# Hybrid attention and convolution layer: bias tiles loaded straight from the tables, convolution steps and bias tables moved to other steps

## The chip, the cores and the metric

One core of one Trainium2 chip runs one program. The metric is device time in microseconds (us), from the first to the last instruction with the little that lies around it; lower is better. Five engines work side by side, each through its own queue in order: TensorE (PE: matmuls; PEld is its weight load), VectorE (DVE), ScalarE (ACT), GpSimd (POOL) and SyncE (SP), which here issues nearly all DMA transfers.

## The reference

One layer over 2048 latent tokens (a grid of 32 rows by 64 columns) and 256 context tokens, width 1024, all in float32:

```python
hx = modulate(rms_norm(x, norm1_g[i]), sh1, sc1)         # hc: the same for ctx
qx, kx, vx, ux = split_proj(hx @ w_in[i])                # 8 heads of 64; u has 1024 columns
attn_x = neighbourhood_attention(rot(qx), qx, rot(kx), vx, kc, vc, rpb[i])
conv_x = conformer_conv(ux, dw_kernel[i], dw_bias[i], conv_ln_g[i], conv_ln_b[i])
x = x + g1 * (concat(attn_x, conv_x) @ w_out[i])
x = x + g2 * (square(relu(modulate(rms_norm(x, norm2_g[i]), sh2, sc2) @ w1)) @ w2)
return rms_norm(x, final_g)
```

Attention: each token sees a window of 8 rows by 16 columns with a learned bias per head (`rpb`, 15 x 31 values a head) and all 256 context keys, in one softmax. Convolution: `a * sigmoid(b)` of u's halves, a depthwise convolution of width 31 over the tokens, a layer norm over 512 channels, silu.

## The kernel before

Every float32 matmul is made of three (`mm3`, L89 to L92): each operand is split into a rounded high part and a low part, high by ScalarE or VectorE, low by a subtraction on VectorE or POOL.

**Projection.** The 2048 tokens are two blocks of 1024, each of two halves of 512 tokens. Each block has ten groups of 256 weight columns: four u groups (they feed the convolution), two q, two k and two v. A step is one group over one half, `half(gi, hf)` at L710; the list at L852 makes 40 steps of them, numbers 0 to 39 (block one: u is 0 to 7, q 8 to 11, k 12 to 15, v 16 to 19; block two the same with 20 more, its v steps interleaved). A q or k step has 48 matmuls of 512 columns; then `rope_store` (L576) rotates its result out of PSUM: VectorE's shuffle (L585) and product (L594), the high and low parts of q and of rotated q (L606, L607, on ScalarE, VectorE and POOL), and eight stores to DRAM. Its tiles come from the ring "G" of four buffers (`gtile`), as do u's gated products, the squares' scratch and the bias tables' tiles.

PSUM is one tile of four slots of 1024 columns. `psA` (L54) hands them out in turn, by the order in which the program is written; one slot is held by the convolution from step 5 on, so three go round. A matmul into a slot waits until all readers of its former content are done. Which ready instruction an engine takes next is fixed when the program is built, by a scheduler with a timing model: program order is the priority, and what isn't ready by the model is passed over.

**Convolution.** 21 blocks of 98 tokens (class `Conv`, L418), each a transform of 128 tokens by matmuls: `load` (cw from h_d), `split`, `fwd` (three matmuls, then y = result x table into the tile cy, its high part cyh on ScalarE and low part cyl on VectorE, L435 to L439), and in the step behind it `inv` (six matmuls, layer norm into co) and two steps behind `turn` (four transposes, silu into ccx, store to cv_d). `conv_end` at a step's end does split and fwd of the present block and loads the next; `conv_at` in the step does turn of the last but one and inv of the last. The blocks 0 to 9 begin at the end of step 7 and go through steps 8 to 16, the blocks 10 to 20 from step 27 to 37. `fwd`'s and `inv`'s results share the held slot.

**Bias tables.** `bias_start` (step 6) spreads rpb in DRAM (z_d). `bias_head` (steps 8 to 15, one a head: q and k of block one) loads two shifted views, adds the column mask on POOL (L287), and stores the head's tables: tf_d has 15 relative rows of 40 columns for 32 query columns, ti_d 14 rows, masked at both ends. `bias_rows(i)` (steps 18, 20, 21, 24) copies from them, DRAM to DRAM, what query row i of four needs, into bias_d: by type of row group (first, middle, last) a [16, 4, 32, n] array, n = 320 or 440. Attention then takes one bias tile, 128 partitions (4 query rows x 32 columns), with one load.

**Attention.** 64 pairs p (4 head pairs `pr` x 8 groups of four grid rows `g` x 2 column halves `hf`), two heads each, in a software pipeline written out by `CYCLE` and `NEED` (L1134, L1141). `addmax` (L1035) adds the bias tile to the scores in PSUM and finds the largest; then exponential, sum, normalising, transposes, product with v. SP's loads are put out by `loads(p)` (L1157): bias and q three pairs ahead, v two, the next head pair's k along the way. A bias tile serves all pairs of one (head pair, hf, type, head): 48 loads in all, 12 a head pair, all at its change, into a ring of eight tiles that come from the weights' ring "W". The outputs go to DRAM (at_d) for the output projection; the MLP follows (from about 990 us on).

**Other pieces the change touches.** `ada_chunk` (L484) makes a modulation row piecemeal on VectorE; its `finish` sums over partitions on TensorE into PSUM, loads the row of b_ada (L517) and adds it (L518). `norm_half` (L545) scales four tiles of x on VectorE and adds the shift on POOL (L221); they are transposed on TensorE (L227) before they can be multiplied.

Of the kernel before, what the change touches and what calls it, by code (L numbers as in the profile page):

```python
# [10 lines left out]
F32 = mybir.dt.float32  # L11
# [7 lines left out]
P = 128  # L19
D = 1024  # L20
# [6 lines left out]
PAD = CW // 2  # L27
# [5 lines left out]
BLK = 1024  # L33
NB = S // BLK

CL = P - CW + 1
# [5 lines left out]
def hybrid_layer(ctx: ExitStack, tc: tile.TileContext, a: dict, out: bass.AP):  # L42
# [68 lines left out]
    ti_d = dr.tile([8, 2, 32, 14 * 40], F32, name="ti_d")  # L111

    bias_d = [dr.tile([16, 4, 32, n], F32, name=f"bias_d{i}") for i, n in enumerate((320, 440, 320))]

# [186 lines left out]

    def bias_rows(i):
        for ty, t, o, n in ((0, tf_d, 7 - i, 320), (1, ti_d, 3 - i, 440), (2, tf_d, 3 - i, 320)):
            SY.dma_start(bias_d[ty][:, i], t.rearrange("h f c n -> (h f) c n")[:, :, o * 40:o * 40 + n])


# [111 lines left out]
    class Conv:  # L418
# [12 lines left out]
        def fwd(self):  # L431
            i, hl, o = self.i, cvc["hl"], cvc["ps"][:, 0:512]
            mm3(o, hl[:, 0, 0:P], hl[:, 1, 0:P], self.w[:, 1, :], self.w[:, 0, :], True, True)
            y = pa.tile([P, 2, 512], F32, tag="acc", bufs=2, name=f"cy{i}")
            VE.tensor_tensor(y, o.unsqueeze(1).broadcast_to([P, 2, 512]), cvc["ab"], ALU.mult)  # L435
            self.yh = pa.tile([P, 2, 512], F32R, tag="H", bufs=3, name=f"cyh{i}")
            self.yl = pa.tile([P, 2, 512], F32R, tag="H", bufs=3, name=f"cyl{i}")
            SE.copy(self.yh, y)
            VE.tensor_tensor(self.yl, y, f(self.yh), ALU.subtract)  # L439
# [24 lines left out]
    cvs = [Conv(i) for i in range(NCB)]  # L464
    cv_pos = [0]

    def conv_at(d, last):
        i = cv_pos[0] - d  # L470
        if 0 <= i < last and not hasattr(cvs[i], f"did{d}"):
            setattr(cvs[i], f"did{d}", True)
            (Conv.inv, Conv.turn)[d - 1](cvs[i])

    def conv_end(last):
        i = cv_pos[0]
        if i < last:
            cvs[i].split()
            cvs[i].fwd()
            if i + 1 < last:  # L480
                cvs[i + 1].load()
        cv_pos[0] += 1

    def ada_chunk(ch):  # L484
# [8 lines left out]
        def step(i):  # L493
# [11 lines left out]
            else:  # L505
                VE.scalar_tensor_tensor(acc, r, sil[:, k:k + 1], acc, ALU.mult, ALU.add)
            if i == 2 * KD:
                pe_todo.append(finish)

        def finish():  # L510
            acc = box["a"]
            pg = psA(f"pg{ch}")
            for n in range(2):
                TE.matmul(pg[0:1, n * 512:(n + 1) * 512], ones[:, 0:1], acc[:, n * 512:(n + 1) * 512],
                          start=True, stop=True)
            br = pa.tile([1, D], F32, tag="m1", bufs=2, name=f"br{ch}")
            SY.dma_start(br, a["b_ada"][:, ch * D:(ch + 1) * D])  # L517
            VE.tensor_tensor(br, pg[0:1, :], br, ALU.add)  # L518
# [26 lines left out]
    def norm_half(tiles, b, hf):  # L545
        scale, shift = norm_mod(tiles, Ar, Br, f"n{b}{hf}")
        for i in range(4):
            scale(i)
            shift(i)
        return tiles  # L550
# [128 lines left out]
    NG = len(groups)  # L679
    CB0 = (BLK - P + PAD) // CL + 1  # L680
    CBS = (CB0, NCB)
    BR0 = 9
    adas = {ch: ada_chunk(ch) for ch in (2, 3, 4)}
    G0 = NG // NB
    ADA = {G0 - 1: 2, G0: 3, G0 + 2: 4}
# [24 lines left out]
    def half(gi, hf):  # L710
# [3 lines left out]
        if kind == "u":  # L714
            ct = idx
            pt = psA(f"pu{b}{ct}{hf}")
            for t in range(4):
                for k in range(KD):
                    wh, wl = wget(k, slice(0, 2 * P))
# [7 lines left out]
            SY.dma_start(h_d[t0:t0 + 512, ct * P:(ct + 1) * P].rearrange("(t p) c -> p t c", p=P), sg)  # L727
            if ct == 3 and hf == 1:
                cv_pos[0] = (0, CB0)[b]
                cvs[cv_pos[0]].load()  # L730
                conv_end(CBS[b])
        elif kind in "qk":
            pt = psA(f"p{kind}{b}{idx}{hf}")
            for j in range(2):
                conv_at(2 - j, CBS[b])
                for k in range(KD):
                    lh, ll = wget(k, slice(j * P, (j + 1) * P))
                    mm3(pt[:, j * 512:(j + 1) * 512], lh, ll, thv[:, k, :], tlv[:, k, :], k == 0, k == KD - 1)
            rope_store(b, kind, idx, hf, pt)
            conv_end(CBS[b])  # L740
        else:
            for t2 in range(2):
# [3 lines left out]
                row = (b * BLK + hf * 512 + t2 * 256) // W  # L746
                conv_at(2 - t2, CBS[b])
                if idx == 1 and hf == 1 and b + 1 < NB:
                    trans_half(pend["x"], b + 1, 0, (2 * t2, 2 * t2 + 1))
                v_tiles([getter(2 * t2), getter(2 * t2 + 1)], row, wget, idx, f"{b}{idx}{hf}{t2}")  # L750
            conv_end(CBS[b])
        if gi == 1 and hf == 0:
# [11 lines left out]
        if gi == 0 and hf == 1:  # L764
# [7 lines left out]
            for i in range(2):  # L772
                scale(i)
                shift(i)
                SY.dma_start(xc_d[i * P:(i + 1) * P, :], ts_[i])
        if gi == 3 and hf == 0:
            bias_start()
            bias_end()
        if 4 <= gi < 8:
            bias_head((gi - 4) * 2 + hf)  # L780
        if gi == 1 and hf == 1:
            conv_loads()
        if gi == 2 and hf == 1:
            conv_tables()
        if hf == 0 and BR0 <= gi < BR0 + 4:
            bias_rows(gi - BR0)
        todo, pe_todo[:] = list(pe_later), list(pe_todo)
# [69 lines left out]
    steps[-4:] = [(NG - 2, 0), (NG - 1, 0), (NG - 2, 1), (NG - 1, 1)]  # L857
    for i, (gi, hf) in enumerate(steps):

        for nxt, nh in steps[i + 1:i + 3]:  # L860
# [137 lines left out]
    def load_b(pr, hf, g, hd):  # L998
# [8 lines left out]
        nw = nr * 40  # L1007
        SY.dma_start(bt[:, SC0 - nw:SC0], bias_d[ty][h * 2 + hf].rearrange("i c n -> (i c) n"))
        BT[key] = bt
# [599 lines left out]
```

## Time and profile before

| | |
|---|---|
| runs | 2570.44, 2568.53, 2560.25 us; median 2568.53 |
| profiled execution | 2570.69 us; span 2568.9 us; mean granted TensorE clock 0.979 |
| PE busy | 2430.5 us (95%) |
| DVE / ACT / POOL busy | 1790.2 (70%) / 1248.7 (49%) / 1467.8 (57%) us |
| DMA | 387.26 MB, mean 151 GB/s |

How to read it: busy time is a sum over the whole span, and TensorE's matmuls overlap, so a busy TensorE isn't one at its peak. The granted clock is the share of TensorE's full clock (2.4 GHz; the lower level is 1.2) in a stretch. Stretches of the span: start and block one's u steps to 158 us, its q steps to about 252, k to 290, v to 348; block two's u to 459, q, k and v to 665; attention to 932.

### The profile page before, as it was taken

How to read it: one execution, taken by the hardware profiler on the slowest of the kernel's cores; microseconds unless marked ns; L12 is line 12 of the kernel's file. 1: busy time of each engine (PE TensorE's matmuls, PEld its weight loads, DVE VectorE, ACT ScalarE, POOL GpSimd, SP SyncE). 2: the span in 40 equal slices, each digit the busy share in tenths (PEclk: the TensorE clock that was granted, in tenths of full speed). 3: DMA queues.
4: the chain of work that ended last, by engine and by line, in shares of the span. 5: the costliest groups of instructions: out<-in, count | busy, mean ns of one | idle time of the engine just before them, and what ended most of it. 6: DMA issues, size and time to landing. Idle time of an engine off the chain costs nothing.

```text
span 2568.9 us, 42313 instructions
## 1 busy us (share of the span) xinstructions
PE 2430.5 (95%) x15903; PEld 2216.9 (86%) x15903; DVE 1790.2 (70%) x2465; ACT 1248.7 (49%) x2162; POOL 1467.8 (57%) x1055
## 2 busy tenths in 40 slices
PE   7997989899889999988999999999999999999997
PEld 5985889689889999987998889999889998799996
DVE  6646743666689976468666697666786676876676
ACT  4334531443689963134444554444554445454442
POOL 3537422442578856457555676555675556755564
PEclk9998999999999999999999999999999999999999
DMA  8555764653899865665333443333343334433321
GB/s 299 158 168 163 223 216 130 196 154 110 227 253 262 241 182 174 195 231 165 99 99 107 129 139 111 101 105 99 121 148 101 99 99 126 137 107 100 105 92 57
DMA packets 293882, 387.26 MB, mean 151 GB/s; under 512 B 38021, under 2 KB 231228, under 8 KB 293644
## 3 DMA queue, kind: packets, MB, share of 16 engines
q1 hardware_dynamic: 293660, 384.54, 49.7%
q8 instruction: 125, 2.05, 0.3%
q14 instruction: 81, 0.66, 0.1%
q10 hardware_dynamic: 16, 0.00, 0.0%
HBM read 308.03 MB, written 86.76 MB: 154 GB/s over the span
## 4 chain that ended last, share of the span: by engine, by line
PE 62%; DVE 10%; DMA 9%; POOL 5%; issue 4%; SPq 2%; ACT 1%; DVEq 0%; POOLq 0%; ACTq 0%
PE pall L90 18%; PE pall L91 18%; PE pall L92 18%; PE pall L1105 2%; PE pall L1069 1%; PE pall L1030 1%; DVE s L1398 1%; DMA ar<-at_d 1%; DVE ac L1501 1%; DVE ac L1497 1%; PE pall L1107 1%; DVE w L1423 1%; PE pall L1032 1%; DMA cw<-h_d 1%; DMA xn_d<-xo 1%
## 5 line engine op out<-in xcount | busy, mean ns | idle before, releaser
L90 PE MATMUL pall<-w,hh 128*128 128x512 f32 x1024 | 406.0, 397 | 11.0 <-DVE ac L1497 7.2
L91 PE MATMUL pall<-w,hh 128*128 128x512 f32 x1024 | 403.0, 394 | 0.0
L92 PE MATMUL pall<-w,hl 128*128 128x512 f32 x1024 | 397.2, 392 | 0.6 <-DVE hl L1454 0.6
L1497 DVE TENSOR_TENSOR ac<-pall,ac 128x1024 f32<-128x1024 f32 x239 | 286.8, 1214 | 73.9 <-PE pall L92 73.2
L90 PEld LDWEIGHTS pall<-w,hh 128*128 128x128 f32 x1024 | 195.1, 190 | 51.6 <-issue 4.4
L92 PEld LDWEIGHTS pall<-w,hl 128*128 128x128 f32 x1024 | 193.3, 189 | 41.9 <-DVE hl L1454 2.2
L91 PEld LDWEIGHTS pall<-w,hh 128*128 128x128 f32 x1024 | 194.8, 190 | 36.4 <-issue 0.2
L1451 ACT ACTIVATE c<-c 128x512 f32<-128x512 f32 x128 | 80.9, 632 | 157.2 <-DVE c L1471 129.2
L86 POOL TENSOR_TENSOR w_0l<-w_0r,w_0h 128x1024 fp32r<-128x1024 f32 x20 | 50.7, 2537 | 172.7 <-ACT w_0h L85 152.5
L90 PE MATMUL pall<-xah,w 128*128 128x256 f32 x512 | 144.8, 284 | 4.7 <-ACT w L1392 4.7
L92 PE MATMUL pall<-xah,w 128*128 128x256 f32 x512 | 145.2, 284 | 0.0
L91 PE MATMUL pall<-xal,w 128*128 128x256 f32 x512 | 145.0, 283 | 0.0
L1454 DVE TENSOR_TENSOR hl<-c,hh 128x512 fp32r<-128x512 f32 x128 | 123.7, 967 | 15.3 <-ACT hh L1453 15.2
L1062 POOL TENSOR_SCALAR sb<-sb,ri 128x696 f32<-128x696 f32 (+1 forms) x128 | 105.6, 826 | 49.7 <-DVE ri L1057 40.7
L1044 DVE CUSTOM_DVE_ANT_0 sb<-pall,bias 128x696 f32<-128x696 f32 (+1 forms) x128 | 108.0, 845 | 6.5 <-PE pall L1032 5.9
L1052 ACT ACTIVATE sb<-sb,mn 128x696 f32<-128x696 f32 (+1 forms) x128 | 109.6, 857 | 0.6 <-DVE mn L1044 0.6
L90 PEld LDWEIGHTS pall<-xah,w 128*128 128x128 f32 x512 | 98.1, 192 | 7.5 <-ACT w L1392 4.9
L91 PEld LDWEIGHTS pall<-xal,w 128*128 128x128 f32 x512 | 98.6, 192 | 2.8
L92 PEld LDWEIGHTS pall<-xah,w 128*128 128x128 f32 x512 | 98.6, 192 | 2.1
L90 PE MATMUL pall<-xth,w 128*128 128x256 f32 x256 | 75.2, 294 | 19.1 <-DVE pu L1459 19.1
L1105 PE MATMUL pall<-pw,v 120*128 120x256 f32 (+1 forms) x480 | 90.8, 309 | 0.8 <-ACT ob L1112 0.8
L1081 DVE TENSOR_TENSOR pw<-pall,pw 120x512 fp32r<-120x512 f32 (+1 forms) x128 | 83.5, 653 | 5.1 <-ACT pw L1076 4.7
(853 smaller groups left out, 8797.0 us busy)
## 6 DMA issues: line engine op xcount, KB each, us to landing
v<-v_d SPq DMA_DIRECT2D x144, 120.0 KB
q<-q_d SPq DMA_DIRECT2D x64, 256.0 KB
wr<-in_w_ada SPq DMA_DIRECT2D x48, 256.0 KB
v_d<-vt SPq DMA_DIRECT2D x64, 160.0 KB
wa<-in_w_ada SPq DMA_DIRECT2D x8, 1024.0 KB
x<-in_x SPq DMA_DIRECT2D x16, 512.0 KB
kr<-k_d SPq DMA_DIRECT2D x32, 256.0 KB
at_d<-ao SPq DMA_DIRECT2D x32, 256.0 KB
```

Of the source, the lines that this page charges most:

```text
L86: (eng or GE).tensor_tensor(l, r, f(h), ALU.subtract)
L90: TE.matmul(outp, lh, rh, start=start, stop=False)
L91: TE.matmul(outp, lh, rl, start=False, stop=False)
L92: TE.matmul(outp, ll, rh, start=False, stop=stop)
L1044: VE.tensor_tensor_reduce(sb[:, c0:SE_], d["s"][:, 512 - SC0 + c0:768], bt[:, c0:SE_], -1.0, 3e38, ALU.add, ALU.min, mn)
L1052: SE.activation(pb[:, c0:SE_], pb[:, c0:SE_], AF.Exp, bias=d["mn"], scale=-1.0, accum_out=d["sm"])
L1062: GE.tensor_scalar(pb[:, c0:SE_], pb[:, c0:SE_], d["ri"], 1.0, ALU.mult, ALU.mult)
L1081: VE.tensor_tensor(pw[0:120, 0:nch, 1, :], d["tv"], f(pw)[0:120, 0:nch, 0, :], ALU.subtract)
L1105: TE.matmul(o, VT[(pr, *key)][0:n, hd, :], pw[0:n, ch, :, :], start=(ch == 0), stop=False)
L1451: SE.activation(c, c, AF.Relu)
L1454: VE.tensor_tensor(dl, cv, f(dh), ALU.subtract)
L1497: VE.tensor_tensor(ac, po_, ac, ALU.add)
```

## The change

1. `bias_d` and `bias_rows` are gone; `load_b` loads a bias tile with four transfers of 32 partitions, one a query row, straight from tf_d or ti_d.
2. `bias_start` and `bias_end` run in step 17 (before: 6), `bias_head` in steps 20 to 27, the u steps of block two (before: 8 to 15).
3. The convolution blocks are put to steps by a table, `ENTER`: blocks 0 to 7 at steps 12 to 19, 8 and 9 at steps 22 and 24, 10 to 20 at steps 27 to 37. u steps call `conv_at` too. The first block's tile is loaded at the end of the step before.
4. `cy` is a PSUM slot by `psA` and no longer an SBUF tile.
5. `ada_chunk` loads its row of b_ada when its last step is put out, not in `finish`.
6. For block two's second half, two of the four shifts of `norm_half` go to VectorE.

```diff
-    bias_d = [dr.tile([16, 4, 32, n], F32, name=f"bias_d{i}") for i, n in enumerate((320, 440, 320))]
-    def bias_rows(i):
-        for ty, t, o, n in ((0, tf_d, 7 - i, 320), (1, ti_d, 3 - i, 440), (2, tf_d, 3 - i, 320)):
-            SY.dma_start(bias_d[ty][:, i], t.rearrange("h f c n -> (h f) c n")[:, :, o * 40:o * 40 + n])
...
-            y = pa.tile([P, 2, 512], F32, tag="acc", bufs=2, name=f"cy{i}")
+            y = psA(f"cy{i}").rearrange("p (z n) -> p z n", z=2)
...
+    now = [0]
+    def conv_at(d):
+        i = ENTER.get(now[0] - d)
+        if i is not None:
             (Conv.inv, Conv.turn)[d - 1](cvs[i])
+    def conv_end():
+        i = ENTER.get(now[0])
+        if i is not None:
             cvs[i].split()
             cvs[i].fwd()
+        i = ENTER.get(now[0] + 1)
+        if i is not None:
+            cvs[i].load()
...
             if i == 2 * KD:
+                box["b"] = pa.tile([1, D], F32, tag="m1", bufs=2, name=f"br{ch}")
+                SY.dma_start(box["b"], a["b_ada"][:, ch * D:(ch + 1) * D])
                 pe_todo.append(finish)
...
-            br = pa.tile([1, D], F32, tag="m1", bufs=2, name=f"br{ch}")
-            SY.dma_start(br, a["b_ada"][:, ch * D:(ch + 1) * D])
+            br = box["b"]
...
-            shift(i)
+            shift(i, VE if b and hf and i % 2 else GE)
...
+    ENTER = {n: i for i, n in enumerate([*range(12, 20), 22, 24, *range(27, 38)])}
...
             for t in range(4):
+                if t % 2 == 0:
+                    conv_at(2 - t // 2)
...
-        if gi == 3 and hf == 0:
+        if gi == G0 - 2 and hf == 1:
             bias_start()
             bias_end()
-        if 4 <= gi < 8:
-            bias_head((gi - 4) * 2 + hf)
+        if G0 <= gi < G0 + 4:
+            bias_head((gi - G0) * 2 + hf)
...
-        if hf == 0 and BR0 <= gi < BR0 + 4:
-            bias_rows(gi - BR0)
...
-        SY.dma_start(bt[:, SC0 - nw:SC0], bias_d[ty][h * 2 + hf].rearrange("i c n -> (i c) n"))
+        t, o = ((tf_d, 7), (ti_d, 3), (tf_d, 3))[ty]
+        for i in range(4):
+            SY.dma_start(bt[i * 32:i * 32 + 32, SC0 - nw:SC0], t[h, hf][:, (o - i) * 40:(o - i) * 40 + nw])
```

## Rows read from the trace of the kernel before

**Rows 1.** Stretches: length, busy us of PE, PEld, DVE, ACT, POOL; clock; DMA.
```profile
185.50:260.00 74.50, 55.83 (x224) 43.36 (x223) 45.68 (x53) 33.45 (x64) 55.40 (x31) 0.84 0.57 161
303.00:348.00 45.00, 41.83 (x340) 40.59 (x339) 19.42 (x32) 19.71 (x36) 4.77 (x2) 1.00 0.96 312
372.00:392.00 20.00, 13.72 (x84) 13.08 (x85) 12.49 (x8) 4.65 (x5) 11.61 (x4) 0.74 0.05 14
...
686.00:726.00 40.00, 40.00 (x321) 39.55 (x320) 39.90 (x100) 37.03 (x80) 34.86 (x50) 1.00 0.98 255
726.00:766.00 40.00, 33.38 (x246) 31.82 (x245) 30.87 (x81) 29.88 (x66) 24.84 (x39) 0.96 1.02 250
790.00:822.00 32.00, 30.61 (x248) 30.18 (x247) 29.69 (x81) 28.88 (x66) 25.23 (x39) 1.00 1.08 253
```

**Rows 2.** Timeline of TensorE, 185 to 262 us: start, length, instruction, [idle before <-releaser].
```profile
202.53 0.50 PE L90 MATMUL pall<-cw,chl 128*128 128x512 f32 x1 [3.26 <-ACT ccx L460]
214.45 0.48 PE L91 MATMUL pall<-cyl,chl 128*98 128x512 f32 x1 [1.51 <-DVE cyl L439]
236.12 0.56 PE L458 MATMUL pall<-ident,co 98*128 98x98 f32 x4 [2.31 <-DVE cy L435]
242.56 0.74 PE L90 MATMUL pall<-cyh,chl 128*98 128x512 f32 x1 [5.09 <-ACT cyh L438]
251.94 0.74 PE L91 MATMUL pall<-cyl,chl 128*98 128x512 f32 x1 [6.50 <-DVE cyl L439]
```

**Rows 3.** Timeline of VectorE in the same stretch.
```profile
234.86 1.20 DVE L435 TENSOR_TENSOR cy<-pall,cab 128x1024 f32<-128x1024 f32 x1
...
242.54 9.34 DVE L439 TENSOR_TENSOR cyl<-cy,cyh 128x1024 fp32r<-128x1024 f32 x1 [5.82 <-ACT cyh L438]
```

**Rows 4.** Timeline of POOL in the same stretch.
```profile
240.18 9.27 POOL L221 TENSOR_TENSOR x<-x,Br 128x1024 f32<-128x1024 f32 x4
```

**Rows 5.** POOL by line, 185.5 to 260 us: busy us, mean ns, idle before.
```profile
L287 POOL TENSOR_TENSOR tb<-tb,cm 64x600 f32<-64x600 f32 x4 | 11.3, 2823 | 5.9 <-DMA cv_d<-ccx 4.5 <-DMA tb<-z_d 1.4
```

**Rows 6.** TensorE's waits, 300 to 395 us: total us, times, longest.
```profile
PE pall L227 <- POOL x L221: 6.3, 3, 2.8
PE pall L90 <- ACT cw L428: 1.8, 1, 1.8
```

**Rows 7.** TensorE's waits, 395 to 660 us.
```profile
PE pall L90 <- DVE br L518: 5.3, 1, 5.3
```

**Rows 8.** Line 230 of the kernel: ns min/median/max, first and last start.
```profile
L230 DVE TENSOR_TENSOR t00l<-pall,t00h x4: 1215/1225/1225, 55.6 to 65.3; 128x1024 fp32r<-128x1024 f32 x4
```

**Rows 9.** Timeline of VectorE, 515 to 541 us, block two's last query half.
```profile
530.87 1.34 DVE L585 STREAM_SHUFFLE sw1q<-pall 128x1024 f32<-128x1024 f32 x1
...
536.94 0.76 DVE L607 TENSOR_TENSOR ql1q<-pall,qh1q 128x256 fp32r<-128x256 f32 x2
```

**Rows 10.** Line 1008, all bias loads on SP's queue: ns min/median/max.
```profile
L1008 SPq DMA_DIRECT2D bias<-bias_d x48: 326/353/1444, 651.9 to 879.2; - x48
```

**Rows 11.** Chain of waits, 720 to 760 us: start, length, what.
```profile
726.85 7.24 DMA bias<-bias_d
734.15 5.08 DMA bias<-bias_d
```

**Rows 12.** Timeline of SP's queue, 726 to 766 us: first, first bias, last row.
```profile
725.43 0.93 SPq L966 DMA_DIRECT2D q<-q_d  x1
726.85 1.64 SPq L1008 DMA_DIRECT2D bias<-bias_d  x2
...
765.81 0.42 SPq L966 DMA_DIRECT2D q<-q_d  x1
```

**Rows 13.** Timeline of SP's queue, 790 to 822 us: first and last row.
```profile
790.15 0.36 SPq L966 DMA_DIRECT2D q<-q_d  x1
...
821.84 0.37 SPq L1123 DMA_DIRECT2D at_d<-ao  x1
```

**Rows 14.** Timeline of SP's queue, 650 to 664 us.
```profile
651.87 2.51 SPq L1008 DMA_DIRECT2D bias<-bias_d  x4
```

More of the change, by code (lines that the diff above doesn't have):

```diff
@@ L464, in hybrid_layer @@
     cvs = [Conv(i) for i in range(NCB)]
[L465 to L472, printed above, removed]
+    now = [0]
+    def conv_at(d):
+        i = ENTER.get(now[0] - d)
+        if i is not None:
             (Conv.inv, Conv.turn)[d - 1](cvs[i])
-    def conv_end(last):
-        i = cv_pos[0]
-        if i < last:
+    def conv_end():
+        i = ENTER.get(now[0])
+        if i is not None:
             cvs[i].split()
             cvs[i].fwd()
-            if i + 1 < last:
-                cvs[i + 1].load()
-        cv_pos[0] += 1
+        i = ENTER.get(now[0] + 1)
+        if i is not None:
+            cvs[i].load()
     def ada_chunk(ch):
@@ L679, in hybrid_layer @@
     NG = len(groups)
-    CB0 = (BLK - P + PAD) // CL + 1
-    CBS = (CB0, NCB)
-    BR0 = 9
+    G0 = NG // NB
+    ENTER = {n: i for i, n in enumerate([*range(12, 20), 22, 24, *range(27, 38)])}
+    assert len(ENTER) == NCB
     adas = {ch: ada_chunk(ch) for ch in (2, 3, 4)}
-    G0 = NG // NB
     ADA = {G0 - 1: 2, G0: 3, G0 + 2: 4}
@@ L727, in half @@
             SY.dma_start(h_d[t0:t0 + 512, ct * P:(ct + 1) * P].rearrange("(t p) c -> p t c", p=P), sg)
[L728 to L731, printed above, removed]
+            conv_end()
         elif kind in "qk":
@@ L734, in half @@
             for j in range(2):
-                conv_at(2 - j, CBS[b])
+                conv_at(2 - j)
                 for k in range(KD):
@@ L739, in half @@
             rope_store(b, kind, idx, hf, pt)
-            conv_end(CBS[b])
+            conv_end()
         else:
@@ L746, in half @@
                 row = (b * BLK + hf * 512 + t2 * 256) // W
-                conv_at(2 - t2, CBS[b])
+                conv_at(2 - t2)
                 if idx == 1 and hf == 1 and b + 1 < NB:
@@ L750, in half @@
                 v_tiles([getter(2 * t2), getter(2 * t2 + 1)], row, wget, idx, f"{b}{idx}{hf}{t2}")
-            conv_end(CBS[b])
+            conv_end()
         if gi == 1 and hf == 0:
@@ L858, in hybrid_layer @@
     for i, (gi, hf) in enumerate(steps):
+        now[0] = i
         for nxt, nh in steps[i + 1:i + 3]:
```

## The prediction

> **What bounds the kernel now.** I read the busy table by stretches first, because the 95% of TensorE on the page is a mean over stages with different limits. Three kinds of stretch touch the change. From 185.5 to 260 us (the first block's query steps) TensorE is busy 55.83 of 74.5 us at a granted clock of 0.84 [rows 1]: the reader is to see a stage that should be bound by TensorE and isn't. From 372 to 392 us (the change of token block) it is busy 13.72 of 20 us at 0.74. From 686 to 726 us (attention at its steady pace) VectorE is busy 39.90 of 40 us, with a hundred instructions, ten per pair: VectorE sets the pace there, 4.0 us a pair. In the MLP behind it nothing is changed, so I look no further.
>
> Then TensorE's own timeline, for who ended its idle time. In the query steps five rows hold 3.26 + 1.51 + 2.31 + 5.09 + 6.50 = 18.7 us, and in all five the matmul that waited or the releaser belongs to the convolution (cw, cyh, cyl, co, ccx) [rows 2]. VectorE's rows say why: cyl, which subtracts two SBUF tiles, took 9.34 us at 242.54, and cy, of the same 128x1024 with one operand in PSUM, took 1.20 us [rows 3]. POOL's timeline has four x additions from 240.18 to 249.45 [rows 4], just the stretch in which cyl stood. Last the chain of waits and SP's queue, for attention's start and the pair at which a new head pair begins.
>
> **The change part by part.** The sum is made against the profiled execution, 2570.69 us (span 2568.9 and 1.8 around it); the median of the three runs is 2568.53, so that execution is 2.2 above it.
>
> (a) Convolution out of the query steps, bias heads out of the query and key steps. The five waits go with the convolution steps that held them. The clock: 0.84 over 74.5 us is 12 us of full-speed time not granted, that is 24 us at the lower of its two levels; the three waits of 236 to 252 take 13.9 us of these, so some 10 us of work ran at half speed and cost 5. Lost in all 18.7 + 5 = 23.7. POOL carries what stays: it was busy 55.40 us in the 74.5, of which the four bias heads were 11.3 [rows 1, 5]. Without them 44 us are left beside some 51 us of TensorE work (55.8 less the 5), so POOL isn't the next bound, but its x additions still queue ahead of query work. I keep 4 us of waits (bounds 0 and 15) and gain 20. The moved convolution costs TensorE the same matmuls elsewhere. Two of the moved steps land in the second block's first-projection steps, with eight bias heads of 2.8 us [rows 5] on a POOL that is lightly loaded there: +1.
>
> (b) The staged copy gone. Twelve DRAM-to-DRAM transfers leave, which stood where the DMA share is 0.96 [rows 1]. Two TensorE waits close by go with them and with the split of the last shift between VectorE and POOL: the cw wait of 1.8 us, and the x waits of 6.3 us [rows 6]. In 372 to 392 us 0.26 x 20 = 5.2 us of clock were not granted, 10 us at the lower level; some 6 of these were work, 3 lost. Gain 1.8 + 6.3 + 3 = 11, of which I take 10 (bounds 3 and 11): after that the second u step's own matmuls are next.
>
> (c) The b_ada row loaded ahead. One wait of 5.3 us, in which VectorE and behind it TensorE stood for a 4 KB load [rows 7], goes.
>
> (d) cy in PSUM. As its subtraction then has one PSUM operand, I price it by the like subtraction t00l, 1.2 us [rows 8]; a VectorE write to PSUM stands in no row, and I bound it by 1.2 and 2.4 us, 21 times, beside TensorE work. It takes one of the three rotating PSUM slots at the end of each conv step, and this is a new wait. I followed the slots through the step list. In the second block the first key half takes the slot that the last query half has only just filled, and the third query half one that cy of the step before filled. In the profile a query half's slot is read from 530.87 (shuffle) to 537.70 (last ql1q) [rows 9]: 6.8 us. Between the two stand only some 2 us of other TensorE work (a conv's forward matmuls and the context's transposes). So 5 us of wait at each of the two: +10, bounds 0 (the scheduler sets another half in front) and 20 (a store holds the reader as well). At the third query half this meets (c)'s wait, so (c) and (d) together are -5.3 + 10 = +5, less 1 for cyl that POOL no longer holds: +4.
>
> (e) Four loads per bias tile in place of one. 48 loads become 192, with the same bytes and rows; all queue on SP, in order, among the q, v, k and output transfers. An issue is 0.326 to 1.444 us, median 0.353 [rows 10]; with the dispatch between two I take 0.40. Each of the three changes of head pair has 12 loads: 36 more issues, 14.4 us. At the first, SP issues for 28.2 of the 40 us (39 rows) and the pace already breaks: the chain there is a bias load of 7.24 us and one of 5.08 behind it [rows 11, 12]. 28.2 + 14.4 = 42.6, so 2.6 us over. At the second, 24.1 of 32 us (32 rows) [rows 13] + 14.4 = 38.5, 6.5 over; the third is like it. Loads run two to three pairs ahead, 8 to 12 us, of which landing takes 5 to 7: I let 4 us of each of the latter two be absorbed, which leaves 2.6 + 2.5 + 2.5 = 7.6. At attention's start 8 loads become 32; SP issued four in 2.51 us there [rows 14], and 24 more are 8 us (at 0.35) to 15 us (at 0.63), of which the gaps in the queue take a part; TensorE's first scores wait for what is behind. I take 4. Together +12; bounds 0 (all in SP's gaps) and 44 (third rival).
>
> The Trainium skill, "DMA: Bandwidth & Descriptors" (Rules for kernel authors), speaks against (e): transfers under 64 KB are mostly overhead. By its fit (Anatomy of one DMA) of 2.0 us plus bytes over 436e3 per us, an estimate for a 160 KB load is 2.4 us, for four 40 KB pieces in a row 8.4. No run here shows pieces of this kind; the rows have 5 to 7 us for a whole load [rows 11], so the trace has the fixed part larger still. By the row the price is the issue alone, as issues don't wait for landings; by the rule, if pieces went in series, it would be the last rival.
>
> **Sum.** -20 + 1 - 10 + 4 + 12 = -13 us: 2557.7 for the profiled execution. Against the median of 2568.5 the same difference gives 2555.5; I forecast 2556.
>
> **Rivals.** *Attention absorbs the pieces.* For it: at its second and third change of head pair TensorE lost little (30.61 busy of 32 us) and SP stands idle a quarter of the time [rows 1, 13]. Against: the first. Without the 12 us: 2544.
>
> *The stall only moves.* The PSUM slot of (d) costs 20 and not 10, or the query steps keep 14 and not 4, since POOL's x additions stay in them. For it: POOL's 9.27 us [rows 4]; against: 44 us of POOL work beside 51. Ten us more: 2566, no change to measure.
>
> *SP becomes attention's bound* (the other side). Place: bias loads of the new head pair, which free their tile only once the old pair's scores are added. If SP has no slack from the first set on, each of the four sets of two loads that VectorE waits for comes 6 x 0.40 = 2.4 us late: 4 x 2.4 x 3 changes = 29, and 15 at the start: 44 in place of 12, 2570.7 - 25 + 44 = 2590, or 2588 by the median. It decides from 25 us on, the sum of the other terms. For it: the 7.24 and 5.08 us on the chain now. Against: at the second change, with the same 12 loads, TensorE is busy 30.61 of 32 us [rows 1].
>
> *Pieces land one after another*, the page's rule as a mechanism. Three more landings of some 5 us [rows 11] for about eight awaited sets: +120, 2666. Against: SP issued two loads in 1.64 us [rows 12] without waiting for a landing.
>
> **How the numbers follow.** Forecast 0.42, absorbed 0.25, moved 0.18, SP 0.13, landing in series 0.02. A measurement of this kernel tells about 0.5% (12.8 us) from no change. The forecast lies at that edge, and I halve it, a little over half to the faster side (0.24); with the absorbed case that makes faster 0.49. The other part of the forecast and the moved case make 0.36 within it. The last two make 0.15 slower. The range from 2534 (absorbed, with nothing kept of the query waits or of (d)) to 2580 (half-way into the SP case) leaves out 1 in 10 to 2 in 10.
>
> **What would show it.** Right: no convolution wait in TensorE's rows of the first block's query steps, a granted clock of 1.00 there and over the change of block, no x wait at that change; a busy share of DMA well under 0.9 in the first block's value steps. (d) shows as a wait of TensorE on ql1q or cyl at the third query half and first key half of block two. (e) shows as 192 bias issues and longer changes of head pair, with the chain running through bias loads. The prediction is wrong if the query steps still lose over 10 us, or if attention's stretch (666 to 932 us now) is longer by over 25 us or by nothing.

## The result, and the profile after

The change made the kernel slower: 2597.76 us (median of 4 runs) against 2569.49, ratio 1.0124, 95% interval 1.0089 to 1.0159. The forecast was 2556, and the range to 2580 did not hold it. Here and below, a head is a bias head, and the slot is the rotating PSUM slot that the change gives to cy.

Three stretches, cut at the start of the first and of the last score addition on VectorE (us of the profiled executions, 2570.69 and 2595.87 us):

| | before | after | |
|---|---|---|---|
| front, to the first | 666.8 | 656.9 | -9.9 (sum of (a) to (d): -25) |
| attention | 262.9 | 299.9 | +37.0 ((e): +12) |
| behind it | 1639.2 | 1637.2 | -2.0 |

So the forecast of -13 us for the profiled execution became +25. Of these 38 us, 25 lie in attention and 15 in the front, less 2 behind it.

Windows of the kernel before over attention, then of the kernel after: length, busy us of PE, PEld, DVE, ACT, POOL; granted clock; DMA share; GB/s.

```profile
666.80:929.70 262.90, 248.41 (x1937) 242.81 (x1936) 242.07 (x620) 229.46 (x500) 205.42 (x301) 0.99 0.92 239
```

```profile
155.40:218.50 63.10, 55.31 (x246) 45.45 (x244) 28.06 (x34) 21.97 (x48) 50.68 (x29) 0.97 0.60 167
259.00:323.00 64.00, 61.20 (x472) 57.85 (x472) 37.91 (x59) 38.60 (x65) 10.81 (x7) 1.00 0.73 226
323.00:362.00 39.00, 32.77 (x246) 31.40 (x245) 22.37 (x21) 22.08 (x34) 14.45 (x6) 0.91 0.37 102
656.90:956.80 299.90, 261.63 (x1938) 253.91 (x1938) 242.35 (x621) 229.98 (x500) 204.71 (x302) 0.94 0.80 210
722.00:764.00 42.00, 29.92 (x193) 28.12 (x191) 23.73 (x64) 23.07 (x53) 20.81 (x33) 0.88 0.78 204
```

The first three lines answer to [rows 1]. The query steps and the first key half have 7.8 us of idle left, all in one wait at the second key half, where [rows 2] has 18.7; the clock is 0.97. In the value steps DMA is at 0.73 where it was 0.96, as forecast, but TensorE had little idle time there to give. The change of block still loses 6.2 of 39 us, at 0.91. The fourth line holds the loss. With as many matmuls, TensorE is busy 13.2 us longer (clock 0.94, was 0.99) and idle 23.8 us longer (299.9 - 261.6 = 38.3, was 14.5). VectorE's work is unchanged. The last line is the first change of head pair, where 12 of 42 us are idle.

Where in attention the 37 us were lost, by the start of score additions on VectorE (two a pair; the head pairs change at pairs 16, 32 and 48):

| first addition of pair | 0 | 8 | 24 | 40 | 56 | last |
|---|---|---|---|---|---|---|
| before | 666.8 | 701.9 | 773.5 | 837.0 | 900.5 | 929.7 |
| after | 656.9 | 698.0 | 778.7 | 853.4 | 927.5 | 956.8 |
| longer by | | 5.9 | 9.2 | 11.1 | 10.6 | 0.1 |

What TensorE and VectorE waited for in attention (655 to 970 us: total, times, longest), in the kernel before,

```profile
DVE kt L842 <- DMA kr<-k_d: 4.2, 1, 4.2
...
PE pall L1030 <- DMA q<-q_d: 2.3, 3, 0.9
```

then in the kernel after:

```profile
PE pall L1025 <- DMA q<-q_d: 20.0, 10, 3.8
```

```profile
DVE kt L833 <- DMA kr<-k_d: 14.3, 4, 6.5
DVE sb L1039 <- DMA v<-v_d: 9.0, 4, 4.2
```

The bias tiles themselves are hardly waited for (3.1 us). SP's queue at the first change shows why q, k and v are, and the line of the bias loads what one costs (ns min/median/max):

```profile
735.77 0.38 SPq L958 DMA_DIRECT2D q<-q_d  x1
736.20 1.45 SPq L982 DMA_DIRECT2D v<-v_d  x3
738.05 5.37 SPq L1003 DMA_DIRECT2D bias<-ti_d  x8
743.52 0.38 SPq L958 DMA_DIRECT2D q<-q_d  x1
...
745.93 3.65 SPq L1003 DMA_DIRECT2D bias<-ti_d  x8
749.68 0.38 SPq L958 DMA_DIRECT2D q<-q_d  x1
```

```profile
L1003 SPq DMA_DIRECT2D bias<-tf_d x128: 302/419/1970, 640.5 to 934.3; - x128
L1003 SPq DMA_DIRECT2D bias<-ti_d x64: 307/419/1714, 661.8 to 896.6; - x64
```

Between two q loads, a pair apart, stand eight bias issues of 5.37 and of 3.65 us in all; a pair has 4.0 us [rows 1], and these three q loads stand 7.75 and 6.16 us apart. SP issues one after another here, so it is late by its own work. A rival is that the bias loads hold the queue because their tile isn't free yet: but from 655 to 955 us SP's queue waited 13 us in all before bias loads, and in the kernel before 16.

### The profile page after: what moved, and what is told of

It reads as the page before. It is cut to its first block, busy times and chain, and to the rows that moved or that the text cites. A ratio compares the mean times of both kernels' runs of the same rounds, so it can differ in the third digit from the quotient of the medians.

```text
span 2594.0 us, 42469 instructions
## 1 busy us (share of the span) xinstructions
PE 2438.3 (94%) x15903; PEld 2225.3 (86%) x15903; DVE 1783.7 (69%) x2467; ACT 1264.5 (49%) x2172; POOL 1457.5 (56%) x1053
## 4 chain that ended last, share of the span: by engine, by line
PE 59%; DVE 12%; DMA 8%; issue 5%; POOL 4%; SPq 2%; ACT 2%; DVEq 0%; POOLq 0%; ACTq 0%
PE pall L90 18%; PE pall L91 18%; PE pall L92 18%; DMA wr<-in_w_ada 1%; DVE s L1393 1%; DMA q<-q_d 1%; DVE ac L1496 1%; PE pall L1064 1%; DMA ar<-at_d 1%; PE pall L1100 1%; DVE ac L1492 1%; DMA kr<-k_d 1%; PE pall L1025 1%; DVE sb L1039 1%; DMA cw<-h_d 1%
## 5 line engine op out<-in xcount | busy, mean ns | idle before, releaser
L90 PE MATMUL pall<-w,hh 128*128 128x512 f32 x1024 | 404.5, 395 | 11.3 <-DVE ac L1492 7.4
L1071 ACT CAST pw<-pall 120x512 fp32r<-120x512 f32 (+1 forms) x128 | 72.6, 567 | 64.9 <-PE pall L1064 51.9
L1064 PE MATMUL pall<-ident,sb 128*120 128x128 f32 x480 | 79.3, 288 | 21.5 <-POOL sb L1057 9.4
```

The lines of the kernel that those rows point to most:

```text
L90: TE.matmul(outp, lh, rh, start=start, stop=False)
L1064: TE.transpose(t[0:120, ch * P:(ch + 1) * P], pb[:, c0 + 120 * ch:c0 + 120 * ch + 120], ident)
L1071: SE.copy(d["pw"][0:120, 0:nch, 0, :], d["tv"])
```

## The experiments

All ratios are to the kernel before in the same session. First is the start of the first score addition in the profiled execution (us); attention is the time from there to the start of the last.

| run | median | ratio, 95% interval | first | attention |
|---|---|---|---|---|
| after | 2597.8 | 1.0124, 1.0089 to 1.0159 | 656.9 | 299.9 |
| e1_one_load | 2578.3 | 1.0032, 1.0014 to 1.0051 | 668.9 | 262.5 |
| e2_before_four | 2600.7 | 1.0132, 1.0093 to 1.0170 | 665.8 | 302.1 |
| e3_before_tiny | 2602.6 | 1.0132, 1.0101 to 1.0162 | 663.1 | 297.0 |
| e4_bias_last | 2603.4 | 1.0128, 1.0094 to 1.0162 | 663.5 | 294.5 |
| e5_staged_late | 2577.5 | 1.0037, 1.0024 to 1.0050 | 670.8 | 264.6 |
| e6_conv_only | 2569.6 | 1.0006, 0.9996 to 1.0016 | 666.8 | 263.6 |
| e7_cy_sbuf | 2593.8 | 1.0095, 1.0080 to 1.0110 | 655.6 | 298.7 |
| e8_no_copy | 2573.8 | 1.0014, 1.0002 to 1.0026 | 665.6 | 265.8 |
| e9_heads_only | 2561.5 | 0.9971, 0.9955 to 0.9987 | 657.1 | 264.0 |
| e10_late_heads_psum | 2579.3 | 1.0040, 1.0026 to 1.0053 | 671.4 | 264.2 |
| e11_late_heads_sbuf | 2574.1 | 1.0020, 1.0009 to 1.0032 | 666.2 | 265.0 |
| e12_heads_and_conv | 2565.2 | 0.9989, 0.9977 to 1.0001 | 654.6 | 267.8 |
| e13_heads_psum | 2579.5 | 1.0049, 1.0031 to 1.0068 | 676.1 | 265.6 |
| e14_heads_br_x | 2564.6 | 0.9987, 0.9975 to 1.0000 | 655.7 | 263.8 |
| e15_x_spread | 2561.6 | 0.9977, 0.9964 to 0.9990 | 652.6 | 265.5 |
| e16_x_spread_conv | 2563.9 | 0.9983, 0.9970 to 0.9996 | 654.2 | 262.1 |

### Attention: e1 to e4

e1, one load per tile in the kernel after:

```diff
+BL, BS = 720, 32 * 720 + 40
+def shifted(t):       # copy i of the table stands 40 columns further on
+    return t.rearrange("(i y) -> i y", i=4)[:, 0:32*BL].rearrange("i (c l) -> c i l", c=32)
...
-SY.dma_start(tf_d[q, hf], src)            # ti_d alike
+SY.dma_start(shifted(tf_d[q, hf])[:, :, 0:600],
+             src.unsqueeze(1).broadcast_to([32, 4, 600]))
...
-for i in range(4):
-    SY.dma_start(bt[i*32:i*32+32, ...], t[h, hf][:, (o-i)*40:(o-i)*40+nw])
+SY.dma_start(bt[:, ...], t[h, hf][0:P*BL].rearrange("(p n) -> p n", n=BL)[:, o*40:o*40+nw])
```

> The kernel after, but a bias tile comes by one load again, still with no staged copy: the tables are stored in DRAM in four copies (one store with a repeated source, so no more stores than in the kernel after), each 40 columns further on, and one load reads all 128 rows. So 48 bias loads in attention in place of 192, all else as in the kernel after. Queue theory (each further issue holds SP's queue, and the q, k and v loads behind it come late): attention's stretch, first to last score addition, goes from 300.6 us back to about 263 (the kernel before), total 2594 - 37 = 2557 us, ratio to the kernel before 0.995. Rival (attention is longer because the front leaves it late tables, queries or values, not because of the pieces): the stretch stays at 290 to 300, total 2585 to 2595, ratio 1.008 or more.

e2, the four pieces in the kernel before:

```diff
-SY.dma_start(bt[:, SC0 - nw:SC0], bias_d[ty][h * 2 + hf].rearrange("i c n -> (i c) n"))
+t, o = ((tf_d, 7), (ti_d, 3), (tf_d, 3))[ty]
+for i in range(4):
+    SY.dma_start(bt[i*32:i*32+32, SC0-nw:SC0], t[h, hf][:, (o-i)*40:(o-i)*40+nw])
```

> The kernel before, but attention's bias tiles come in four pieces from the tables; the staged copy is still made and not read. Queue theory: attention's stretch goes from 263 to about 300 us, total 2569 + 37 = 2606, ratio 1.0145; the front unchanged. Rival (the front's new order is what makes attention long): stretch 263 to 270, total 2569 to 2576, ratio up to 1.003.

e3, tiny loads beside the one load in the kernel before:

```diff
+for i in range(3):
+    SY.dma_start(bt[i * 32:i * 32 + 32, 760:800], tf_d[h, hf][:, 0:40])
```

> The kernel before with its one load per bias tile, and behind each three more tiny loads (32 rows of 160 bytes) into a part of the tile that nothing reads: as many issues on SP as with four pieces, with hardly any bytes more. Queue theory: the issues alone cost it, attention's stretch 290 to 300 us, total 2596 to 2606, ratio 1.011 to 1.0145. Rival (the pieces cost by their size or where they read, each a transfer of 40 KB with 32 rows, not by their number): stretch under 270, total under 2576, ratio under 1.003.

e4, the order in `loads(p)` of the kernel after:

```diff
-if p + 3 < NP:                            # first
-    for hd in range(2):
-        load_b(*groups_[p + 3], hd)
...
+if p + 3 < NP:                            # last, behind load_kc
+    for hd in range(2):
+        load_b(*groups_[p + 3], hd)
```

> The kernel after with its four pieces, but in each pair's loads the bias pieces stand behind the q, v, k and context loads of the same pair, not ahead of them. Queue theory as the trace of after reads (q and kr stand behind bias issues and are what attention waits for): those waits shrink from 20.0 and 14.3 us to under 8 each, attention's stretch 270 to 285 us, total 2565 to 2580. Third rival as the prediction put it (the bias tiles themselves are late, since their tile comes free late): the waits turn into waits of VectorE for bias, stretch 295 or more, total 2590 or more.

Attention's window (columns as above) in e1,

```profile
668.90:931.40 262.50, 249.69 (x1937) 244.46 (x1936) 241.85 (x620) 228.82 (x500) 205.03 (x301) 0.97 0.90 239
```

in e2,

```profile
665.80:967.90 302.10, 260.92 (x1936) 253.60 (x1935) 241.95 (x620) 229.92 (x499) 204.55 (x301) 0.94 0.81 209
```

and in e3:

```profile
663.10:960.10 297.00, 260.67 (x1937) 253.24 (x1937) 243.28 (x620) 229.44 (x499) 204.89 (x301) 0.93 0.81 214
```

Undone, the pieces give all 37 us back. Alone they cost 39, and 144 loads of 5 KB behind whole tiles cost 34. So it is nearly all the number of loads, and size and place are worth 5 us at most; the front's order is ruled out. In e3 too the largest wait of TensorE is for q (20.1 us), which nothing of the tiny loads touches but the queue. Pieces that land in series, the prediction's last rival at +120 us, are ruled out by the 39. The rule of the Trainium skill that stood beside that rival ("DMA: Bandwidth & Descriptors", Rules for kernel authors: under 64 KB one pays mostly overhead) fits e3 against e2 in so far as the size hardly mattered. The fit that the prediction took from the same page of the Trainium skill is given there for transfers that GpSimd issues, and these go through SP; no run here shows it. Nor do [rows 11] show a larger fixed part: their 5 to 7 us are whole loads, in a stretch where the DMA engines were busy throughout [rows 1].

e1's total missed by 21 us: its front is 12 us longer than after's. More on that below.

In e4 VectorE waits for bias instead (its waits, 655 to 965 us: total, times, longest):

```profile
DVE kt L833 <- DMA kr<-k_d: 17.1, 4, 6.4
...
DVE sb L1039 <- DMA bias<-ti_d: 7.1, 6, 2.4
...
DVE sb L1039 <- DMA bias<-tf_d: 5.4, 6, 1.9
```

TensorE's waits for q halve to 10.5, kr's do not fall, 12.5 us of bias waits appear, and attention is 5 us shorter. Who is late is a matter of order; that somebody is late is not. The queue theory's size failed; the third rival's size nearly came out (294.5 us against 295 or more), but its reason, late bias tiles, only in part.

### The front: e5 to e16

e5, the copy late in the kernel after, with the one load from `bias_d`:

```diff
+if hf == 0 and G0 + 5 <= gi < G0 + 9:
+    bias_rows(gi - (G0 + 5))
```

> The kernel after with the staged copy made again, but in the second block's last query, key and first value steps, where the DMA share of the kernel after is 0.36 to 0.62, and with one load per bias tile. Queue theory: attention's stretch is back at 263 us (300.6 with four pieces), and the front stays within 4 us of the kernel after, so 2594 - 37 = 2557 to 2561 us, ratio to the kernel before 0.995 to 0.997. Rival (the staged copy itself costs the 10 us that step (b) of the prediction gave it, wherever it stands): the front is 8 to 12 us longer than in the kernel after, 2565 to 2569, ratio 0.998 to 1.000.

Attention is back, but the front is 14 us longer than after's, worse than the rival said. The first row of TensorE's waits, 60 to 660 us:

```profile
PE pall L90 <- ACT cw L428: 16.8, 2, 16.2
```

A convolution input (cw) stands behind the copies: SP issued eleven of them from 463 to 482 us, cw's load at 482.3, and the DMA engines were busy 90% or more from 466 to 500 us. So here the copy holds TensorE up for 16 us, and its price depends on where it stands.

e6, the convolution's places in the kernel before:

```diff
-CB0 = (BLK - P + PAD) // CL + 1
-CBS = (CB0, NCB)
+ENTER = {n: i for i, n in enumerate([*range(12, 20), 22, 24, *range(27, 38)])}
...                                        # conv_at, conv_end as in the kernel after
```

> The kernel before with one part of the change alone: the convolution's steps in the places that the kernel after gives them (off the first block's queries, two in the second block's first-projection steps). Bias heads, staged copy, cy and b_ada stay as before. Step (a) as the prediction sized it: 20 us less, less what the four bias heads left beside the queries hold (some 3): 2552 us, ratio 0.993. What the trace of after says (18.7 us of waits go from the queries, 7.8 us of one new wait stand there, and the moved convolution's waits come up in the second block): 8 to 12 us less, 2557 to 2561, ratio 0.995 to 0.997.

e7, cy in the kernel after:

```diff
-y = psA(f"cy{i}").rearrange("p (z n) -> p z n", z=2)
+y = pa.tile([P, 2, 512], F32, tag="acc", bufs=2, name=f"cy{i}")
```

> The kernel after with cy in SBUF again, not in a rotating PSUM slot; else the kernel after. Step (d) as the prediction sized it (slot waits of 10 us, 1 us won on cyl): 9 us less than after, front 648 us, total 2585. What the trace of after says (no wait there has a slot's reader as its releaser for more than some 3 us, and cyl took 1.2 us each time where before it took up to 9.3 us beside POOL): 0 to 8 us more, front 657 to 665, total 2594 to 2602.

e8, no copy in the kernel before, with e1's tables and load:

```diff
-if hf == 0 and BR0 <= gi < BR0 + 4:
-    bias_rows(gi - BR0)
```

> The kernel before without the staged copy: the tables stand in DRAM four times, each 40 columns further on (stored in the first block's query and key steps, no more stores than before), and one load per bias tile reads all 128 rows. Step (b) as the prediction sized it, with the x split left out: front 667 - 8 to 10 = 657 to 659 us, total 2559 to 2561, ratio 0.996. What the trace of after says (x had landed early and its scaling on VectorE and POOL was what TensorE waited for, copy or not): the front moves by no more than 3 us, 664 to 669, total 2566 to 2571, ratio 0.999 to 1.001.

None of the prediction's three prices came out here. e6: no gain. e8: no gain, rather 0.1% slower; but the fourfold stores stand in its query and key steps, so it doesn't tell what the copy's removal is worth alone. e7 is 4 us faster than after by the medians, with the sign of (d) but not its 9 us, and the two intervals overlap. What e7's expectation read from the trace of after was wrong: the wait of 7.8 us there, with ql0q as its releaser, is a wait for a slot's reader (below).

e9 is e8 with the heads moved (`bias_start` and `bias_end` too, to step 17):

```diff
-if 4 <= gi < 8:
-    bias_head((gi - 4) * 2 + hf)
+if G0 <= gi < G0 + 4:
+    bias_head((gi - G0) * 2 + hf)
```

> The kernel of the run without the staged copy (before, tables in DRAM four times, one load per bias tile), with one more part of the change: the eight bias heads stand in the second block's first-projection steps, as in the kernel after, not in the first block's query and key steps. Convolution, cy and b_ada as before. Step (a) as the prediction sized it: the heads' share is small (some 3 us of the 20 in the queries, +1 in the second block), 2571 us, within 3 of that run's 2573.75. Rival (the heads' additions on POOL and their stores on SP are the larger part of (a); moving the convolution alone gave nothing): the first block is 8 us or more shorter, total under 2566.

12 us less than e8 by the medians, as the rival said; in the profiles 8.5 us of it are in the front (665.6 to 657.1) and 1.8 in attention. This run beats both kernels.

e10 is e1 with the heads later, and e11 is e10 with e7's edit too:

```diff
-if G0 <= gi < G0 + 4:
-    bias_head((gi - G0) * 2 + hf)
+if G0 + 5 <= gi < G0 + 9:
+    bias_head((gi - G0 - 5) * 2 + hf)
```

> The kernel after with one load per bias tile (tables in DRAM four times), and the bias heads eight steps or more later: second query group, both key groups and the first value group of the second block, where the DMA share of the kernel after is 0.36 to 0.62. Theory (what was lost between the kernel after's front and that of the run with one load, 12 us, are the fourfold table stores and the heads on SP's queue among the projection's and the ada weights' loads): front 657 to 660, attention 263, total 2557 to 2562, ratio 0.996. Rival (the convolution's and the queries' chains on VectorE and ScalarE set the second block, whatever stands on SP): front 668 to 671 as there, total 2575 to 2578.

> The kernel of the run before this one (one load, late bias heads), with cy in SBUF as in the kernel before. The run with cy in SBUF alone won 3 to 4 us on the kernel after: so 2553 to 2559 us, ratio 0.994 to 0.996, if that gain is the PSUM slot's; the same as the run before this one if it was chance.

e10 came out at its rival's numbers (671.4 and 2579.3), and e11 missed: heads still later are no better. Attention's first addition comes 9 us after the last value half's matmuls in e11, 3 in the kernel after and e7; TensorE waits 7.5 us of it for the first q load. cy in SBUF is 5 us better, as in the pair e7 and after.

e12, e13 and e14 each add one part of the change to e9: e12 the edit of e6, e13 that of e7 the other way round, e14

```diff
+    box["b"] = pa.tile([1, D], F32, tag="m1", bufs=2, name=f"br{ch}")     # in step
+    SY.dma_start(box["b"], a["b_ada"][:, ch * D:(ch + 1) * D])
...
-shift(i)
+shift(i, VE if b and hf and i % 2 else GE)
```

> The run with late bias heads (before, no staged copy, one load per tile, heads beside the second block's first projections), with the convolution also moved as in the kernel after; cy in SBUF, b_ada and x as before. Step (a) as the prediction summed it (what the convolution's five waits in the queries cost is won by moving it): 14 to 20 us less than that run's 2561.5, so 2542 to 2548. Rival, from the run with the convolution alone moved (its waits come up again in other steps, and in the second block it meets the heads' stores on SP's queue): 2561 to 2572, no gain or a loss.

> The run with late bias heads, with cy in a rotating PSUM slot, as in the kernel after; all else as there. Step (d) as the prediction sized it: 2561.5 + 10 - 1 = 2570. From the pair of runs that differ in cy alone (3 to 4 us): 2565. Rival (cyl, 6.2 us of waits there, is won and no slot is waited for): 2556 to 2560.

> The run with late bias heads, with b_ada loaded ahead and the last shift of x split between VectorE and POOL, as in the kernel after. The prediction's sizes (5.3 for the b_ada row and, in step (b), 6.3 for the x waits, split and copy together): 2550 to 2553. From the trace of after (x waits of 7.2 us shrink to 4.5 + 2.1, and the wait for the b_ada row turns into one for the adaptive row's sum on VectorE): 0 to 3 less, 2558 to 2562.

e12: no gain, as its rival said. e13: 18 us lost, more than any of the three numbers expected. e14: no gain in its 12 runs (its profiled run, 2556.7, is the lowest of them). e12 differs from e1 by (c), (d) and the x split, and its front is 14 us shorter (654.6 against 668.9). As e14 shows no gain from (c) and the split, that points to the slot, together with the fourfold stores: the kernel after has the slot without them and a front of 656.9. e12 against e8 is the whole of (a), heads and convolution: 9 us by the medians, 6 by the ratios, where the prediction had 19.

e15 and e16 cut the scaling of x in two, on e9 and on e12:

```diff
-if b + 1 < NB and kind == "q" and idx == 1 and hf == 0:
-    norm_half(pend["x"], b + 1, 0)
+if b + 1 < NB and kind == "q" and idx == 1:
+    if hf == 0:
+        pend["n"] = norm_mod(pend["x"], Ar, Br, f"n{b + 1}0")
+    for i in range(2 * hf, 2 * hf + 2):
+        for fn in pend["n"]:
+            fn(i)
```

> The run with late bias heads, with the scaling and shifting of the second block's first four x tiles cut in two: two tiles after the second query group's first half as before, the other two after its second half. Theory (the query steps' long stall is that work itself, 12 us on VectorE beside POOL's additions; which instruction is queued behind it, convolution or query, is by chance): the one stall of 8.6 us there falls below 4, the front is 4 to 6 us shorter, total 2555 to 2558. Rival (the stall is the convolution's own chain between the engines): 2561 to 2562, no change.

> The same cut on the run that also moves the convolution (2565.2). Theory: the query steps of that run have no convolution, and what waits there for x's work is a query step; total 2559 to 2562. Rival: no change, 2564 to 2566.

In e15's trace the stall shrinks (below), but its time is the rival's, no change. In e16 the cut did not take the work apart: VectorE took the second two scalings 0.4 us after the first two, and the stall went from 4.3 to 3.9 us. So e16 tests nothing.

## Why the prediction was wrong

**(e) was mis-sized: 12 us, measured 37 (34 to 39 by e1 to e3).** Its 4 us for attention's start were nearly right (5.9 measured). Its 7.6 us for the three changes of head pair were not: they cost 9.2, 11.1 and 10.6. Four things were wrong in the step. It set SP's issues against 40 us as a whole, where eight bias issues stand between two q loads and a pair has 4.0 us. It let 4 us at two of the changes be absorbed by loads that run ahead; but they run ahead in the same queue, and a queue that is behind absorbs nothing. It looked for the victim in the bias tiles, while q, k and v wait in the queue too and are wanted as soon. And it had no term for the clock: of the 37 us, 13.2 are TensorE's own work, slower at 0.94. The step's 0.40 us per issue was about right (median 0.419). The third rival, SP as attention's bound, named the cause and gave 44 and 2588; I gave it 0.13. Its changes were sized right (29 us, measured 31), its start was not (15, measured 5.9), and its path was not either: it had the bias tiles come late. That its 29 is so near is luck in part.

**(a) failed: 20 us expected from five waits, 6 to 9 measured (e12 against e8), none of them from the convolution's move.** It took the instruction that waited for the one that cost. The timelines tell it (start, length, instruction, [idle before <-releaser]). VectorE in e6,

```profile
213.26 13.79 DVE L218 SCALAR_TENSOR_TENSOR x<-x,n10ss,Ar 128x1024 f32<-128x1024 f32 x4
```

and in e9:

```profile
218.33 12.38 DVE L219 SCALAR_TENSOR_TENSOR x<-x,n10ss,Ar 128x1024 f32<-128x1024 f32 x4
```

TensorE's longest wait of that stretch in e6,

```profile
229.97 0.75 PE L90 MATMUL pall<-cyh,chl 128*98 128x512 f32 x1 [10.79 <-ACT cyh L438]
```

in e9,

```profile
235.56 0.92 PE L461 MATMUL pall<-ident,co 98*128 98x98 f32 x4 [8.56 <-DVE co L455]
```

in the kernel after,

```profile
218.46 0.80 PE L90 MATMUL pall<-t01h,w_0h 128*128 128x512 f32 x1 [7.79 <-DVE ql0q L601]
```

and in e7, which is the kernel after with cy in SBUF:

```profile
223.50 0.75 PE L90 MATMUL pall<-cyh,chl 128*98 128x512 f32 x1 [4.16 <-ACT cyh L432]
```

In each of these VectorE scales the four tiles of the next block's x there, and one stall follows: on cyh, on co, or on the query's own ql0q. In the kernel before, the last late row of [rows 2] is of the same kind, since POOL's additions of x [rows 4] slowed cyl [rows 3]. The row before it, 5.09 us for cyh, hung on a bias head: POOL's addition of the head's mask took 6.42 us beside the scaling (its line stands in the last section), POOL's sum m10q came behind it, and ScalarE took q's parts before cyh. POOL, then ScalarE, in the kernel before:

```profile
237.88 2.33 POOL L598 TENSOR_TENSOR m10q<-m10q,sw0q 128x1024 f32<-128x1024 f32 x1
```

```profile
240.24 1.32 ACT L606 CAST qh0q<-m10q 128x256 fp32r<-128x256 f32 x4 [4.90 <-POOL m10q L598]
241.47 1.04 ACT L438 CAST cyh<-cy 128x1024 fp32r<-128x1024 f32 x1
```

The convolution was the victim in both. Moved away, with the heads gone too, it leaves a stall of 4.3 us there (e12) in place of 8.6 (e9), but waits come up in other steps. In e6 these are ACT ccx 6.3 and cw 4.7 in TensorE's waits to 660 us, beside cyh's 10.8. Windows of e9,

```profile
200.00:260.00 60.00, 51.44 (x225) 41.49 (x225) 48.09 (x51) 30.85 (x56) 43.42 (x22) 0.91 0.55 154
260.00:650.00 390.00, 363.37 (x2402) 326.66 (x2401) 215.82 (x269) 155.60 (x259) 145.55 (x81) 0.96 0.60 175
```

and of e12:

```profile
200.00:260.00 60.00, 55.24 (x254) 44.89 (x254) 52.58 (x48) 24.48 (x41) 44.28 (x20) 0.97 0.49 138
260.00:650.00 390.00, 359.05 (x2389) 321.26 (x2388) 225.62 (x291) 175.71 (x288) 136.52 (x78) 0.96 0.61 176
```

TensorE is idle 3.8 us less up to 260 us and 4.3 us more behind it. With the scaling cut in two, VectorE's timeline of e15 has

```profile
216.17 5.75 DVE L219 SCALAR_TENSOR_TENSOR x<-x,n10ss,Ar 128x1024 f32<-128x1024 f32 x2
223.64 4.89 DVE L219 SCALAR_TENSOR_TENSOR x<-x,n10ss,Ar 128x1024 f32<-128x1024 f32 x2
```

and TensorE's

```profile
224.51 0.67 PE L90 MATMUL pall<-cyh,chl 128*98 128x512 f32 x1 [2.65 <-ACT cyh L441]
231.91 0.47 PE L91 MATMUL pall<-cyl,chl 128*98 128x512 f32 x1 [2.12 <-DVE cyl L442]
```

4.8 us of stall in place of 8.6. That the scaling is the cause of this stall is thus shown in one pair of traces; that it is worth time in the whole is not. What did gain, some 12 us, is the move of the heads (e9 against e8). The step counted them as POOL's load (11.3 us, 44 us left beside 51) and not as what held the chain to cyh. How these 12 divide between POOL and SP stays open.

**(b) failed.** The x waits that were to go with the copy stay in the kernel after (TensorE, 270 to 365 us),

```profile
PE pall L225 <- DVE x L219: 4.5, 1, 4.5
PE pall L225 <- POOL x L219: 1.8, 1, 1.8
```

6.3 us as before [rows 6]: the releasers are the scaling and shifting of x, and they are late without a copy beside them too. The split between VectorE and POOL only changed the releaser. The clock at the change of block, 3 us of the step, did not come back to 1.00 either (0.91). The DMA share of the value steps fell as forecast, and nothing hung on it. What the copy's removal is worth alone no run tells.

**(c) and (d): no gain seen, and a price without one value.** The 5.3 us of the b_ada row were worth nothing that shows. In e9, which still loads it late, the wait for it is gone, and one of 5.6 us for the adaptive row's sum on VectorE stands at 435 us, 64 us ahead of the old place; in e14, which loads it early, that one is 6.0. e7 loads it early too and still waits 2.8 us at the old place for the row's addition on VectorE, so the load was only part of that wait. The slot wait of (d) is real. In e13 it is at one of the two places where it was put, TensorE's at block two's third query half:

```profile
505.10 0.80 PE L90 MATMUL pall<-t10h,w_0h 128*128 128x512 f32 x1 [6.87 <-DVE cyl L442]
```

In the kernel after it is at neither (0.5 us for cyl there). It is in block one, where the step didn't look: the stall of 7.79 us on ql0q above. With three slots going round, the second key half comes three after the last query half as soon as cy takes one between them, so it gets that half's slot and must wait for ql0q, VectorE's reading behind the scaling of x. e1, e5 and e10, which share both, have the same wait (7.5 to 7.7 us). With cy back in SBUF (e7, e11, e12) it is gone, and the stall there is 4.2 to 4.3 us on cyh. e13 against e9 prices (d) at 18 us, e10 against e11 at 5, after against e7 at 4, which isn't clear of noise; I had 9, bounds to 20. Why it is dear in e13, cheaper in e10 with fourfold stores too, and cheap in the kernel after stays open.

**Sum.** The front's terms were not independent. Several waits hung on one cause, and with one removed others came up: 25 us of terms gave 9.9. The heads' 12 us less the slot's 4, by the runs above, come near it, though no run shows that these two add up.

## What to carry to other kernels

Before counting a wait as won, ask what its releaser was itself doing and who stands behind it; waits near one long instruction can be one wait. Count the issues of an in-order queue against the time of the shortest stretch that needs them, for every load in it, and take a queue that is behind as lost for all of them. When a buffer joins a rotation, follow every later user of the rotation and not only those of one stage. A table stored with a repeated source in shifted copies gives one load where four would be needed; a head takes no more stores for it, but four times the bytes, and the masked ends take 16 stores in place of 4 (e1).

## What the hardware showed

Scaling a 128x1024 tile by a column and a row on VectorE took 1.27 us at this place of the kernel before and 2.9 on average in the kernel after, where POOL added beside it (3.4 on average in e6, where one of the four took 9.4). VectorE's timeline of the kernel before,

```profile
229.41 4.86 DVE L218 SCALAR_TENSOR_TENSOR x<-x,n10ss,Ar 128x1024 f32<-128x1024 f32 x4
```

of the kernel after,

```profile
206.30 11.77 DVE L216 SCALAR_TENSOR_TENSOR x<-x,n10ss,Ar 128x1024 f32<-128x1024 f32 x4
218.00 0.74 DVE L601 TENSOR_TENSOR ql0q<-pall,qh0q 128x256 fp32r<-128x256 f32 x2
```

and POOL's of the kernel before, then of the kernel after:

```profile
229.16 6.42 POOL L287 TENSOR_TENSOR tb<-tb,cm 64x600 f32<-64x600 f32 x1
...
253.13 1.46 POOL L287 TENSOR_TENSOR tb<-tb,cm 64x600 f32<-64x600 f32 x1
```

```profile
210.39 9.91 POOL L219 TENSOR_TENSOR x<-x,Br 128x1024 f32<-128x1024 f32 x3
```

The Trainium skill, "SBUF — State Buffer" (Who interferes with whom), states that a VectorE instruction with two SBUF inputs contends with a GpSimd instruction that reads SBUF, and that the one which comes second waits. The rows agree that the two contend: in the kernel before POOL waited, its addition taking 6.42 us where the same took 1.46 elsewhere, and in the kernel after VectorE did, with ql0q behind it, while POOL's additions of x took 3.3 us each (2.3 in [rows 4]). That the second one waits they don't show: POOL's row of 6.42 us starts 0.25 us ahead of VectorE's first scaling. With an operand in PSUM cyl took 1.2 us all 21 times in e13, with both in SBUF up to 9.34 [rows 3].
